# A decoder layer on one core: FFN groups that ran ahead alternate with others, a transposed row of scales through DRAM, B11 kept where T1 will stand, and the last product in single banks

## The chip, the cores and the metric

The kernel runs on one core of one Trainium2 chip. The metric is the device time of one execution in microseconds (us). Engines are named as the profile names them: PE (TensorE, matmuls; PEld its weight loads), DVE (VectorE), ACT (ScalarE), POOL (GpSimd), SP (SyncE, which only issues DMAs here).

## The reference

The layer works on 1024 tokens of width 1024 in float32.

```python
h = rmsnorm(x, pre_mix_g[l])
z = jnp.einsum('btd,dc->btc', h, w_in[l])
q_p, f_p, i_p, g_p, gate_b, gate_c, conv_h = jnp.split(z, split_pts, axis=-1)
mix_a = hgrn2_mixer(q_p, f_p, i_p, g_p, lb_all[l], hgrn_norm_g[l])
mix_b = gate_b * causal_dwconv(gate_c * conv_h, conv_w[l])
mix = jnp.einsum('btc,cd->btd', jnp.concatenate([mix_a, mix_b], axis=-1), w_out[l])
x = x + rmsnorm(mix, post_mix_g[l])
h = rmsnorm(x, pre_ffn_g[l])
u = causal_dwconv(jnp.einsum('btd,df->btf', h, ffn_w_up[l]), ffn_conv_w[l])
gate, val = jnp.split(u, 2, axis=-1)
y = jnp.einsum('btf,fd->btd', jax.nn.silu(gate) * val, ffn_w_down[l])
x = x + rmsnorm(y, post_ffn_g[l])
```

`rmsnorm` multiplies each token by the reciprocal root of its mean square and by a gain. The FFN has 2816 gate and 2816 value columns.

## The kernel before

**Precision.** Every float32 operand of a matmul is split into a high part (a cast, on ACT as a rule, L113) and a low part (a subtraction, on DVE, L114). A product is then three matmuls: high by high, low by high, high by low (`mm3_fm` L167 to L169, `mm3_tm` L172 to L174). Names that begin with h are high parts, those with l low parts.

**Mixing stages, in two halves of 512 tokens.** `gemm_quad` computes four feature tiles of a projection at once in four PSUM banks of pool `ps_mm`: first f0 (forget gate of half 0), then q0, i0, g0, the convolution branch `z_conv` and so on. The scale of each token (`rstd`, a chain of small DVE operations L147 to L155) is not needed before the banks are read out: `evac_f` multiplies each bank of f0 by `rb`, the scales spread over all partitions. For half 0, `stats_by_feature` sums squares with matmuls into `pc`, `rstd` follows, and `by_token` spreads the four columns of scales: four diagonal matrices `dg` on DVE, four matmuls `pb` on PE, one copy `rb` on ACT. These `pb` matmuls stand inside the f0 product. POOL casts the masks `m_diag` and `m_lev` meanwhile. For half 1, `stats` sums squares on ACT and `by_token_through_dram` writes the scales to DRAM and reads them back in transposed order, both on SP.

**FFN up.** It is a Strassen-Winograd scheme over 22 groups of columns, each with seven products. The function `head_1` and `head_2` compute the first two; for the eight groups of `AHEAD` these were computed earlier (`ahead`) and `take_back` loads the result. The other five products are named here by their left operands c2, c1, c7, c4 and c3 (`c2h` the high part). The products c2, c1 and c7 of a group all read one right operand `t` of three parts (`h_t`, `l_t`), which has a single buffer; c4 and c3 read `h_b`, `l_b`. Each product is 12 matmuls. The gate half gathers in PSUM tile `pG`, the value half in `pV`. After c2 and after c7 ACT copies the gate half to `s` (L749), which is added to `pV` on DVE; c4 writes over the place that the second copy reads. The loop at L893 runs one group's `take_back` or `head_1`, then of the group before c4 (`tail_1`), then `head_2`, then c3 (`tail_2`), then c2, c1, c7 of the group (`mid`). `AHEAD = 8` means groups 0 to 7.

**FFN down.** Again seven products, in the order 1, 2, 6, 7, 5, 3, 4, over 22 rows of 128 of which each product sees 11, cut into six granules `GR` of two rows or one. `down_granule` loads the left operand `s` and `right_operand` the right one; blocks B11, B12, B21, B22 of the weight come from `w_dn`, and T1 = B12 - B11, T2 = B22 - T1, T3 = B22 - B12 are made on DVE. The first two granules of product 1 (`EARLY`) were made before. Products alternate between the four banks `bx` and the four banks `by`. Within a granule the row blocks c go (0, 1), then (2, 3). Product 4 is the last; its last three granules are `joined`, so that blocks 0 and 1 end before blocks 2 and 3.

**The end.** `result` squares a block on ACT (`jy`) and multiplies it by the gain on DVE (`my`); `finish_rows` runs `rstd` over the blocks it is given and adds the residual (L1037), then SP stores.

The order of instructions on each engine is fixed when the program is built: a list scheduler places them from the code's order and its own estimates, and `tc.high_priority()` moves a part forward.

Of the kernel before, what the change touches and what calls it, by code (L numbers as in the profile page):

```python
# [17 lines left out]
P = 128  # L18
# [23 lines left out]
def decoder_kernel(ctx: ExitStack, tc: tile.TileContext, x, xT, w_sq, w_cv, w_out, w_up, w_dn,  # L42
# [27 lines left out]
    nc.vector.tensor_scalar(neg[:], vec[:, V_PREF : V_PREF + KH], -1.0, None, ALU.mult)  # L70
# [414 lines left out]
    def z_conv(hf, act, rb, rates, at_end):  # L485
        res = []
        rates = list(rates)
        for j in range(4):
# [23 lines left out]
            if j == 3 and at_end is not None:  # L512
                at_end()
# [99 lines left out]

    first = {}

    def scale_a():
        for _ in hgen:
            pass
        nc.sync.dma_start(ident[:], ident_d)
        with tc.high_priority():  # L620
            first["r"] = stats_by_feature()

    def scale_a_rows():
        with tc.high_priority():
            first["rows"] = by_token(0, first["r"])
# [26 lines left out]
    def ma_tiles(hf):  # L652
# [44 lines left out]
    AHEAD = 8  # L697
# [149 lines left out]
    ahead((AHEAD - 1, 0), {0: box[0]["f"]})  # L847
# [87 lines left out]
    def raw_w(kh, nh, i, n, name):  # L935
        t = ft("wr", (P, 2, TH), name, 5)
# [6 lines left out]
    def t_1(gi, n, b11, b12):  # L943
        t = ts[1, gi] = t_slot(1, gi, n)
        nc.vector.tensor_tensor(t[:], b12[:, :n], b11[:, :n], ALU.subtract)

    def right_operand(op, gi, i, n):

        nm = f"{op}_{gi}"
        if op == 1:  # L950
            b = raw_w(0, 0, i, n, f"b11_{nm}")
            t_1(gi, n, b, raw_w(0, 1, i, n, f"b12_{nm}"))
            return b
        if op == 2:
# [16 lines left out]
        return ts[{5: 1, 6: 2, 7: 3}[op], gi]  # L971
# [163 lines left out]
```

## Time and profile before

| | |
|---|---|
| median of 3 runs | 1138.54 us (1137.28 to 1140.52) |
| the profiled execution | 1138.99 us, of which its span is 1137.2 us |
| mean granted TensorE clock | 0.994 of full |
| PE busy | 1109.6 us, 98% of the span |
| DVE, ACT, POOL busy | 838.4, 512.6 and 9.7 us |
| chain that ended last | PE 86%, DVE 6%, DMA 3%, ACT 3%, issue 2% |

Times in the trace count from the start of the span. Busy time of PE counts a matmul from its start to its modelled end, and these overlap; what PE loses is therefore read from the distance between two starts, and from idle time in front of an instruction together with what ended it.

### The profile page before, as it was taken

What the parts mean: (1) busy time and instruction counts of PE and PEld (TensorE: products, weight loads), DVE (VectorE), ACT (ScalarE), POOL (GpSimd) and SP (SyncE); (2) the same over time, 40 slices, a digit from 0 to 9 for tenths busy, and PEclk for the clock granted to TensorE, in tenths of its full rate; (3) what the DMA queues carried; (4) which work ended last, traced back from release to release, by engine and by line L of the source; (5) the groups of instructions that cost most, each with busy time, mean ns of one, the idle gap of its engine ahead of it and who ended that gap; (6) DMA issues with size and microseconds to landing.
All of it is one profiled execution on the core that took longest, in us unless ns stands there. A gap on an engine that the chain in (4) does not pass through costs nothing.

```text
span 1137.2 us, 13444 instructions
## 1 busy us (share of the span) xinstructions
PE 1109.6 (98%) x5096; PEld 912.8 (80%) x5096; DVE 838.4 (74%) x1181; ACT 512.6 (45%) x750; POOL 9.7 (1%) x16
## 2 busy tenths in 40 slices
PE   8999999999999999999999999999999999999996
PEld 6878888888878888887777888888888877888884
DVE  8578767636687777387998987878887777744786
ACT  6543335425432337366555444444444433544441
POOL 2000000000000000000000000000000000000000
PEclk9999999999999999999999999999999999999998
DMA  8522223335322238174444323222331479735653
GB/s 292 172 78 74 75 93 113 119 95 201 101 66 86 82 111 260 59 256 167 164 168 168 111 94 139 102 75 102 131 110 51 153 282 334 280 102 168 202 165 132
DMA packets 54432, 163.03 MB, mean 143 GB/s; under 512 B 5856, under 2 KB 6112, under 8 KB 51424
## 3 DMA queue, kind: packets, MB, share of 16 engines
q1 hardware_dynamic: 53936, 161.57, 41.5%
q8 instruction: 40, 0.66, 0.2%
q10 hardware_dynamic: 432, 0.61, 0.2%
q14 instruction: 24, 0.20, 0.1%
HBM read 127.82 MB, written 34.34 MB: 143 GB/s over the span
## 4 chain that ended last, share of the span: by engine, by line
PE 86%; DVE 6%; DMA 3%; ACT 3%; issue 2%; DVEq 0%; SPq 0%; ACTq 0%
PE pG L167 8%; PE pG L169 8%; PE pG L168 8%; PE pV L167 4%; PE pV L169 4%; PE pV L168 4%; PE sl L382 2%; PE p_wo L174 2%; PE p_wo L173 2%; PE p_wo L172 2%; DMA b<-w_dn 2%; PE pXv L173 2%; PE pXv L174 1%; PE pXv L172 1%; PE p_ch L169 1%
## 5 line engine op out<-in xcount | busy, mean ns | idle before, releaser
L113 ACT CAST hs<-s 128x1024 fp32r<-128x1024 f32 (+1 forms) x40 | 39.1, 976 | 91.9 <-PE pXg L173 35.9
L114 DVE TENSOR_TENSOR ls<-s,hs 128x1024 fp32r<-128x1024 f32 (+1 forms) x40 | 45.2, 1129 | 44.4 <-ACT hs L113 44.2
L114 DVE TENSOR_TENSOR l_b<-w,h_b 128x1024 fp32r<-128x1024 f32 x22 | 26.9, 1223 | 33.6 <-ACT h_b L113 33.6
L167 PE MATMUL pG<-uhi,h_x 128*128 128x512 f32 x112 | 44.4, 396 | 0.0
L168 PE MATMUL pG<-ulo,h_x 128*128 128x512 f32 x112 | 44.3, 395 | 0.0
L169 PE MATMUL pG<-uhi,l_x 128*128 128x512 f32 x112 | 44.1, 394 | 0.0
L749 ACT COPY s<-pG 128x512 f32<-128x512 f32 x44 | 25.7, 583 | 40.8 <-PE pG L169 40.6
L114 DVE TENSOR_TENSOR l_t<-t,h_t 128x1536 fp32r<-128x1536 f32 x22 | 38.6, 1755 | 5.9 <-ACT h_t L113 5.7
L811 ACT ACTIVATE g<-pG,vec 128x1024 f32<-128x1024 f32 x22 | 24.5, 1116 | 34.2 <-PE pG L169 34.2
L167 PE MATMUL pG<-c4h,h_b 128*128 128x512 f32 x88 | 35.4, 402 | 4.7 <-ACT s L749 4.7
L820 ACT ACTIVATE g<-g 128x1024 f32<-128x1024 f32 x22 | 23.3, 1061 | 36.3 <-DVE g L813 36.1
L113 ACT CAST h_t<-t 128x1536 fp32r<-128x1536 f32 x22 | 32.6, 1484 | 14.4 <-DVE t L783 9.6
L113 ACT CAST h_x<-w 128x1024 fp32r<-128x1024 f32 x14 | 14.7, 1052 | 47.4 <-DMA w<-w_up 47.4
L383 DVE COPY_PREDICATED S<-m_lev,sl 128x512 f32<-128x512 uint8 x28 | 24.9, 890 | 14.7 <-PE sl L382 14.7
L369 ACT COPY lhs<-UW 128x512 f32<-128x512 f32 x28 | 18.6, 663 | 37.2 <-DVE UW L390 37.2
L382 PEld LDWEIGHTS sl<-UW,lhs 128*128 128x128 f32 x224 | 28.8, 190 | 7.3 <-issue 4.1
L169 PE MATMUL pG<-c4h,l_b 128*128 128x512 f32 x88 | 34.6, 393 | 0.0
L167 PE MATMUL pV<-c3h,h_b 128*128 128x512 f32 x88 | 34.5, 392 | 0.0
L167 PE MATMUL pG<-c7h,h_t 128*128 128x512 f32 x88 | 34.4, 391 | 0.1
L169 PE MATMUL pV<-c3h,l_b 128*128 128x512 f32 x88 | 34.4, 391 | 0.0
L169 PE MATMUL pG<-c7h,l_t 128*128 128x512 f32 x88 | 34.3, 390 | 0.0
L168 PE MATMUL pG<-c4l,h_b 128*128 128x512 f32 x88 | 34.3, 390 | 0.0
(351 smaller groups left out, 3524.1 us busy)
## 6 DMA issues: line engine op xcount, KB each, us to landing
w<-w_up SPq DMA_DIRECT2D x22, 1024.0 KB, 4.8
s<-s_d SPq DMA_DIRECT2D x33, 512.0 KB, 3.9
b<-w_dn SPq DMA_DIRECT2D x33, 512.0 KB, 6.0
s_d<-g SPq DMA_DIRECT2D x22, 512.0 KB, 2.9
s_d<-S SPq DMA_DIRECT2D x11, 768.0 KB, 3.4
r_wo<-w_out SPq DMA_DIRECT2D x16, 512.0 KB, 3.5
xT<-xT SPq DMA_DIRECT2D x16, 256.0 KB, 4.0
r_q<-w_sq SPq DMA_DIRECT2D x8, 512.0 KB, 4.3
```

Source lines behind the costliest of these rows:

```text
L113: nc.scalar.copy(hi, src)
L114: nc.vector.tensor_tensor(lo, src, hi.bitcast(F32), ALU.subtract)
L167: nc.tensor.matmul(ps, whi, ahi, start=first, stop=False, skip_group_check=more)
L168: nc.tensor.matmul(ps, whi, alo, start=False, stop=False, skip_group_check=more)
L169: nc.tensor.matmul(ps, wlo, ahi, start=False, stop=last, skip_group_check=more)
L172: nc.tensor.matmul(ps, ahi, whi, start=first, stop=False, skip_group_check=more)
L173: nc.tensor.matmul(ps, ahi, wlo, start=False, stop=False, skip_group_check=more)
L174: nc.tensor.matmul(ps, alo, whi, start=False, stop=last, skip_group_check=more)
L382: nc.tensor.matmul(pv[:, :, i], lhs[:, i, :], rhs, start=True, stop=True)
L383: nc.vector.copy_predicated(view(S, 2 * X, o + h, (X - h, 2), (2 * h, n), (1, h)), m_lev[:, li].rearrange("p x g (b h) -> p x (g b) h", h= ...
L749: nc.scalar.copy(t[:], ps)
L811: nc.scalar.mul(a[:], c, wc[2])
```

## The change

1. **Scales by token.** `by_token` now transposes the four columns of scales on PE in one matmul (`pc<-ident,rs_x`), copies the 4x128 result on ACT, writes it to DRAM on ACT's DMA queue and reads it back to all partitions on POOL's. The product q0 stands in banks of the other pool (`banks=aux`), and `evac_f` is called from inside it. The masks load after the third weight tile of q0. `stats(1)` moves into `z_conv`.
2. **FFN up.** The groups computed ahead are 0, 1, 3, 5, 7, 9, 11, 13; where the next group is one of them, the code writes c3 and then c4 of the group before, without a head between.
3. **FFN down.** Product 1 loads B11 alone, into the slot of T1; product 2 loads B12 and B21 and subtracts in place; T2 is made in product 6 and T3 in product 7, from blocks loaded there again. `wr` has 8 buffers for 5, `sr` 6 for 4. `bx` is all of pool `ps_g`, `by` all of `ps_v`.
4. **The end.** Product 4 adds up in four single banks `pZ`, into which ACT first copies `s3`; its last four granules are joined, and each row block is finished by itself (`last_rows`). `finish_rows(0)` is written ahead of product 4.

```diff
-    def by_token(hf, r):
-
-        pb = aux(f"pb{hf}", (P, NC_H, C))
-        dg = cv(f"dg{hf}", shape=(P, NC_H, C))
-        for c in range(NC_H):
-            nc.vector.tensor_scalar(dg[:, c, :], ident[:], r[:, c : c + 1], None, ALU.mult)
-            nc.tensor.matmul(pb[:, c, :], ones[:], dg[:, c, :], start=True, stop=True)
+    def by_token(hf, r, ps):
+
+        nc.tensor.transpose(ps, r[:], ident[:])
+        t = zt("rt", (NC_H, C), name=f"rt{hf}")
+        nc.scalar.copy(t[:], ps)
+        rd = dp.tile([NC_H, C], F32, name=f"rd{hf}")
+        nc.scalar.dma_start(rd, t[:])
         rb = zt("rb", (P, TH), name=f"rb{hf}")
-        nc.scalar.copy(rb[:], pb.rearrange("p c t -> p (c t)"))
+        nc.gpsimd.dma_start(rb[:], rd.rearrange("c p -> (c p)").partition_broadcast(P))
         return rb
...
-    pss = gemm_quad(w_sq[0], Lazy(), "f0", False, (1, 1, 1, 1, 1, 1, 1, 1), pieces=2, queue=nc.scalar,
-                    hooks={6: scale_a, 7: scale_a_rows})
+    def scale_a_rows():
+        nc.scalar.activation(warm[:], first["r"][:, 0:1], AF.Sigmoid)
+        first["FU"] = evac_f(0, pss, first["rows"])
+
+    pss = gemm_quad(w_sq[0], Lazy(), "f0", False, (1, 1, 1, 1, 1, 1, 1, 1), pieces=2, queue=nc.sync,
+                    hooks={6: scale_a})
     r0 = first["r"]
+    qss = gemm_quad(w_sq[1], act_a, "q0", False, PAIRS, hooks={0: scale_a_rows}, banks=aux)
...
-    AHEAD = 8
+    AHEAD = (0, 1, 3, 5, 7, 9, 11, 13)
...
         if n and not last:
             mid_weights(n)
-        if n:
-            tail_1(n - 1)
-        if n >= AHEAD and not last:
-            head_2(n)
-        if n:
-            tail_2(n - 1)
+        if n and n in AHEAD:
+            product_3(n - 1)
+            product_4(n - 1)
+            gate(n - 1)
+            value(n - 1)
+        elif n:
+            product_4(n - 1)
+            gate(n - 1)
+            if not last:
+                head_2(n)
+            product_3(n - 1)
+            value(n - 1)
...
+        if op <= 2 and (op == 1) == (gi >= EARLY):
+            ts[1, gi] = t_slot(1, gi, n)
+            nc.sync.dma_start(ts[1, gi][:], w_dn[0, 0, :, i : i + n])
         if op == 1:
-            b = raw_w(0, 0, i, n, f"b11_{nm}")
-            t_1(gi, n, b, raw_w(0, 1, i, n, f"b12_{nm}"))
-            return b
+            return ts[1, gi]
         if op == 2:
             b = raw_w(1, 0, i, n, f"b21_{nm}")
             b12 = raw_w(0, 1, i, n, f"b12_{nm}")
-            if gi < EARLY:
-                t_1(gi, n, raw_w(0, 0, i, n, f"b11_{nm}"), b12)
+            nc.vector.tensor_tensor(ts[1, gi][:], b12[:, :n], ts[1, gi][:], ALU.subtract)
+            return b
+        if op == 6:
             b22 = raw_w(1, 1, i, n, f"b22_{nm}")
-            t2 = ts[2, gi] = t_slot(2, gi, n)
-            t3 = ts[3, gi] = t_slot(3, gi, n)
-            nc.vector.tensor_tensor(t2[:], b22[:, :n], ts[1, gi][:], ALU.subtract)
-            nc.vector.tensor_tensor(t3[:], b22[:, :n], b12[:, :n], ALU.subtract)
+            ts[2, gi] = t_slot(2, gi, n)
+            nc.vector.tensor_tensor(ts[2, gi][:], b22[:, :n], ts[1, gi][:], ALU.subtract)
+            return ts[2, gi]
+        if op == 7:
+            b12 = raw_w(0, 1, i, n, f"b12_{nm}")
+            b = raw_w(1, 1, i, n, f"b22_{nm}")
+            nc.vector.tensor_tensor(b[:, :n], b[:, :n], b12[:, :n], ALU.subtract)
             return b
...
-            for cs in ((0, 1), (2, 3)):
+            for cs in ((0,), (1,), (2,), (3,)) if len(gis) > 1 else ((0, 1), (2, 3)):
...
+                if len(gis) > 1 and done:
+                    done(cs[0])
...
-    down_product(4, bx, joined=3)
     finish_rows(0, range(NC_H))
-    for cs in ((0, 1), (2, 3)):
-        for c in cs:
-            result(1, 0, c, bx[c])
-        finish_rows(1, cs)
+
+    def last_rows(c):
+        result(1, 0, c, bz[c])
+        finish_rows(1, [c])
+
+    down_product(4, bz, joined=4, done=last_rows)
```

How this stands in the instruction streams is shown at three places. The first is PE in FFN up, at the end of the c7 product of group 2, with its `pG` (`pG_4533` before, `pG_4537` in the change); `h_t_4670` and `l_t_4671` are the right operand of group 3, `h_b_4630` and `h_b_4656` belong to group 2. Before:

```order
L167 MATMUL pG_4533<-c7h,h_t_4541 128x512
L168 MATMUL pG_4533<-c7l,h_t_4541 128x512
L169 MATMUL pG_4533<-c7h,l_t_4542 128x512
L167 MATMUL pG_4533<-c4h,h_b_4630 128x512
L168 MATMUL pG_4533<-c4l,h_b_4630 128x512
L169 MATMUL pG_4533<-c4h,l_b_4631 128x512
```

In the change:

```order
L167 MATMUL pG_4537<-c7l,h_t_4555 128x512
L168 MATMUL pG_4537<-c7h,l_t_4556 128x512
L166 MATMUL pG_4662<-c2h,h_t_4670 128x512
L167 MATMUL pG_4662<-c2l,h_t_4670 128x512
L166 MATMUL pV_4708<-c1h,h_t_4670 128x512
L166 MATMUL pG_4537<-c4h,h_b_4656 128x512
L167 MATMUL pG_4537<-c4l,h_b_4656 128x512
L168 MATMUL pG_4537<-c4h,l_b_4657 128x512
L166 MATMUL pV_4613<-c3h,h_b_4656 128x512
```

Two c2 matmuls and one c1 matmul of group 3 now stand directly behind the last c7 matmul of group 2, ahead of c4 and c3 of group 2. The same three stand there between groups 4 and 5, 6 and 7, 8 and 9, 10 and 11, and 12 and 13; between 0 and 1 c4 follows c7 as before, and between an odd group and the next even one 12 head matmuls stand ahead of c4.

The second place is ACT at the same point of the program, with the two copies `s` and the cast `h_t` of the next group. Before (groups 2 and 3):

```order
L749 COPY s_2_4600<-pG_4533 128x512
L820 ACTIVATE g_4557<-g_4557 128x1024
L776 COPY pG_4636<-f_4634 128x1024
L749 COPY s_2_4627<-pG_4533 128x512
L113 CAST h_t_4644<-t_4640 128x1536
```

In the change (groups 4 and 5; `h_x` is the operand of the head of group 6):

```order
L112 CAST h_b_4880<-w_4755 128x1024
L741 COPY s_4_4850<-pG_4761 128x512
L112 CAST h_t_4894<-t_4890 128x1536
L741 COPY s_4_4877<-pG_4761 128x512
L112 CAST h_x_4981<-w_4979 128x1024
```

The cast `h_t` of the next group now stands ahead of the second copy instead of behind it.

The third place is DVE towards the end, in product 4: the residual sums of half 0 (`my`, with `xr`) and the low parts of the last two granules (`ls_4`, `lw_4`, `ls_5`, `lw_5`). Before:

```order
L1037 SCALAR_TENSOR_TENSOR my_1_7167<-my_1_7167,rs_y_8499,xr_8523 128x512
L1037 SCALAR_TENSOR_TENSOR my_2_7168<-my_2_7168,rs_y_8499,xr_8527 128x512
L114 TENSOR_TENSOR ls_4_8418<-s_4_8412,hs_4_8417 128x1024
L114 TENSOR_TENSOR lw_4_8422<-b_4_4_8414,hw_4_8421 128x1024
L1037 SCALAR_TENSOR_TENSOR my_2_7168<-my_2_7168,rs_y_8499,xr_8531 128x512
L1037 SCALAR_TENSOR_TENSOR my_3_7169<-my_3_7169,rs_y_8499,xr_8535 128x512
L1037 SCALAR_TENSOR_TENSOR my_3_7169<-my_3_7169,rs_y_8499,xr_8539 128x512
L114 TENSOR_TENSOR ls_5_8431<-s_5_8425,hs_5_8430 128x1024
L114 TENSOR_TENSOR lw_5_8435<-b_4_5_8427,hw_5_8434 128x1024
```

In the change:

```order
L1045 SCALAR_TENSOR_TENSOR my_2_7152<-my_2_7152,rs_y_8305,xr_8337 128x512
L1045 SCALAR_TENSOR_TENSOR my_3_7153<-my_3_7153,rs_y_8305,xr_8341 128x512
L1045 SCALAR_TENSOR_TENSOR my_3_7153<-my_3_7153,rs_y_8305,xr_8345 128x512
L113 TENSOR_TENSOR ls_4_8455<-s_4_8449,hs_4_8454 128x1024
L113 TENSOR_TENSOR lw_4_8459<-b_4_4_8451,hw_4_8458 128x1024
L113 TENSOR_TENSOR ls_5_8468<-s_5_8462,hs_5_8467 128x1024
L113 TENSOR_TENSOR lw_5_8472<-b_4_5_8464,hw_5_8471 128x1024
```

All eight residual sums of half 0 now stand ahead of the low parts of both granules, where five of them stood ahead of the first pair and three ahead of the second.

## Rows read from the trace of the kernel before

**Rows 1.** The page: busy us (share) xinstructions; a DMA group's KB, us to landing.

```profile
PE 1109.6 (98%) x5096; PEld 912.8 (80%) x5096; DVE 838.4 (74%) x1181; ACT 512.6 (45%) x750; POOL 9.7 (1%) x16
...
b<-w_dn SPq DMA_DIRECT2D x33, 512.0 KB, 6.0
```

**Rows 2.** Waits of PE: waiter, waited for, us in total, times, longest.

```profile
PE pG L167 <- ACT s L749: 4.7, 7, 0.7
...
PE pb L278 <- DVE dg L277: 1.9, 1, 1.9
```

**Rows 3.** Windows: length, busy us (instructions) of each engine, PE clock, DMA share, GB/s.

```profile
925.00:980.00 55.00, 51.74 (x214) 40.31 (x213) 41.84 (x39) 23.45 (x28) 0.00 (x0) 0.97 0.94 352
980.00:1126.00 146.00, 146.00 (x646) 120.81 (x644) 91.47 (x119) 62.71 (x88) 0.00 (x0) 1.00 0.50 159
...
955.00:960.00 5.00, 4.58 (x13) 3.63 (x14) 4.43 (x6) 1.24 (x2) 0.00 (x0) 0.66 0.83 267
...
26.00:36.00 10.00, 8.13 (x40) 6.57 (x39) 7.35 (x17) 8.87 (x14) 2.02 (x5) 1.00 0.85 287
```

**Rows 4.** Timeline of PE around `pb`: start us, length us, instruction, [idle before].

```profile
26.16 0.39 PE L168 MATMUL p_f<-lo,h_f 128*128 128x512 f32 x1
...
26.61 0.39 PE L167 MATMUL p_f<-hi,h_f 128*128 128x512 f32 x1
28.87 1.16 PE L278 MATMUL pb<-dg,ones 128*128 128x128 f32 x8 [1.87 <-DVE dg L277]
29.78 0.48 PE L168 MATMUL p_f<-lo,h_f 128*128 128x512 f32 x1
```

**Rows 5.** Timeline of DVE and POOL there: the chain of `rstd` of half 0, mask casts.

```profile
23.75 0.16 DVE L147 TENSOR_SCALAR rt_x<-pc 128x4 f32<-128x4 f32 x1
23.95 0.52 DVE L150 TENSOR_SCALAR rs_x<-rt_x 128x4 int32<-128x4 int32 x1
...
28.53 0.88 DVE L277 TENSOR_SCALAR dg<-ident,rs_x 128x128 f32<-128x128 f32 x4 [0.33 <-DVE rs_x L155]
...
23.84 3.96 POOL L642 CAST m_lev<-mf 128x512 uint8<-128x512 f32 x7
```

**Rows 6.** Timeline of DVE: first and last of the ten operations of `rstd`, half 1.

```profile
42.14 0.16 DVE L147 TENSOR_SCALAR rt_x<-ssx 128x4 f32<-128x4 f32 x1
...
43.92 0.16 DVE L155 SCALAR_TENSOR_TENSOR rs_x<-rt_x,rs_x 128x4 f32<-128x4 f32 x1
```

**Rows 7.** Timeline of PE and ACT between two FFN groups (one of seven alike).

```profile
590.23 0.39 PE L169 MATMUL pG<-c7h,l_t 128*128 128x512 f32 x1
...
590.66 0.58 ACT L749 COPY s<-pG 128x512 f32<-128x512 f32 x1 [2.92 <-PE pG L169]
591.14 1.49 ACT L113 CAST h_t<-t 128x1536 fp32r<-128x1536 f32 x1
...
591.29 0.50 PE L167 MATMUL pG<-c4h,h_b 128*128 128x512 f32 x1 [0.68 <-ACT s L749]
```

**Rows 8.** Timeline of the end: last matmul, ACT, DVE.

```profile
1125.91 0.39 PE L174 MATMUL pXg<-hw,ls 128*128 128x512 f32 x1
...
1127.19 0.68 DVE L1022 TENSOR_TENSOR my<-pXg,pg 128x512 f32<-128x512 f32 x1
...
1129.24 0.16 DVE L147 TENSOR_SCALAR rt_y<-ssy 128x2 f32<-128x2 f32 x1
...
1131.40 2.74 DVE L1037 SCALAR_TENSOR_TENSOR my<-my,rs_y,xr 128x512 f32<-128x512 f32 x4
```

**Rows 9.** Timeline of DVE and ACT in product 4.

```profile
1094.50 1.28 DVE L1024 TENSOR_TENSOR my<-pYv,ds 128x512 f32<-128x512 f32 x2
...
1105.92 3.40 DVE L1037 SCALAR_TENSOR_TENSOR my<-my,rs_y,xr 128x512 f32<-128x512 f32 x5
1109.24 1.22 DVE L114 TENSOR_TENSOR ls<-s,hs 128x1024 fp32r<-128x1024 f32 x1
...
1107.07 1.06 ACT L113 CAST hs<-s 128x1024 fp32r<-128x1024 f32 x1 [4.29 <-PE pXg L173]
```

More of the change, by code (lines that the diff above doesn't have):

```diff
@@ L184, in gemm_quad @@
     def gemm_quad(src, act, name, token_major, groups, order=None, pieces=1, rate=1, hooks=None, queue=None,
-                  gains=None):
+                  gains=None, banks=None):
         order = order or list(range(len(act)))
-        pss = [ps_mm.tile([P, TH], F32, tag="mm", name=f"p_{name}_{j}") for j in range(4)]
+        pss = [banks(f"p_{name}_{j}") if banks else ps_mm.tile([P, TH], F32, tag="mm", name=f"p_{name}_{j}")
+               for j in range(4)]
         ws, i0 = {}, 0
@@ L511, in z_conv @@
             psb = gemm_tile(w_cv[3 * j + 2], act, f"gb{n}")
-            if j == 3 and at_end is not None:
-                at_end()
+            if at_end and j >= 2:
+                at_end[j - 2]()
             tick(rates.pop(0))
@@ L612, in __getitem__ @@
             return act_a[k]
+    lbt = zp.tile([P, 4, H], F32, name="lbt")
+    lbp = vec[:, V_LB : V_LB + H]
+    e_, s_, lb, oml = (lbt[:, i, :] for i in range(4))
+    nc.vector.tensor_tensor(e_, lbp, lbp, ALU.subtract)
+    nc.scalar.activation(e_, e_, AF.Exp)
+    nc.vector.reciprocal(s_, e_)
+    nc.vector.tensor_tensor(s_, s_, e_, ALU.mult)
+    nc.vector.tensor_tensor(lb, s_, s_, ALU.subtract)
+    nc.vector.tensor_scalar(oml, lb, -1.0, 1.0, ALU.mult, ALU.add)
     first = {}
@@ L620, in scale_a @@
         with tc.high_priority():
-            first["r"] = stats_by_feature()
+            pc = aux("pc", (P, NC_H + P))
+            for c in range(NC_H):
+                nc.tensor.matmul(pc[:, c : c + 1], sums[0][:, c * C : (c + 1) * C], ones[:, 0:1], start=True, stop=True)
+            first["r"] = rstd(pc[:, :NC_H], D, "x0")
+            first["rows"] = by_token(0, first["r"], pc[:NC_H, NC_H:])
     def scale_a_rows():
-        with tc.high_priority():
-            first["rows"] = by_token(0, first["r"])
-    pss = gemm_quad(w_sq[0], Lazy(), "f0", False, (1, 1, 1, 1, 1, 1, 1, 1), pieces=2, queue=nc.scalar,
-                    hooks={6: scale_a, 7: scale_a_rows})
+        nc.scalar.activation(warm[:], first["r"][:, 0:1], AF.Sigmoid)
+        first["FU"] = evac_f(0, pss, first["rows"])
+    pss = gemm_quad(w_sq[0], Lazy(), "f0", False, (1, 1, 1, 1, 1, 1, 1, 1), pieces=2, queue=nc.sync,
+                    hooks={6: scale_a})
     r0 = first["r"]
-    rb0 = first["rows"]
+    qss = gemm_quad(w_sq[1], act_a, "q0", False, PAIRS, hooks={0: scale_a_rows}, banks=aux)
+    rb0, (F0, UW0) = first["rows"], first["FU"]
     rq0 = for_values(0, r0)
-    F0, UW0 = evac_f(0, pss, rb0)
-    pss = gemm_quad(w_sq[1], act_a, "q0", False, PAIRS)
-    evac_q(0, pss, rb0, UW0)
+    evac_q(0, qss, rb0, UW0)
     for i in range(2):
@@ L715, in ahead @@
                     nc.sync.dma_start(f_d[n], to[i])
-    for n in range(1, AHEAD - 1, 2):
-        ahead((n, n + 1), {})
+    for i in (1, 3, 5):
+        ahead(AHEAD[i : i + 2], {})
     tick(len(fill))
@@ L846, in decoder_kernel @@
     mid_weights(0)
-    ahead((AHEAD - 1, 0), {0: box[0]["f"]})
+    ahead((AHEAD[-1], 0), {0: box[0]["f"]})
     comb = (P, KH, TH)
@@ L890, in decoder_kernel @@
     ps_v = ctx.enter_context(tc.tile_pool(name="ps_v", bufs=2, space=PSUM, reuse_waits="tile"))
-    ps_g = ctx.enter_context(tc.tile_pool(name="ps_g", bufs=2, space=PSUM, reuse_waits="tile"))
+    scope_g = ExitStack()
+    ps_g = scope_g.enter_context(tc.tile_pool(name="ps_g", bufs=2, space=PSUM, reuse_waits="tile"))
     for n in range(NF + 1):
         last = n == NF
-        if n >= AHEAD and not last:
+        if n not in AHEAD and not last:
             head_weights(n)
             head_1(n)
-        elif n < AHEAD:
+        elif not last:
             take_back(n)
@@ L1057, in decoder_kernel @@
     s3 = keep(bx, "ds3_")
+    scope_g.close()
+    ps_d = ctx.enter_context(tc.tile_pool(name="ps_d", bufs=4, space=PSUM, reuse_waits="tile"))
+    bz = [ps_d.tile([P, TH], F32, tag="mm", name=f"pZ{c}")[:] for c in range(NC_H)]
+    for c in range(NC_H):
+        nc.scalar.copy(bz[c], s3[c][:])
     down_product(5, by, True)
```

68 lines of the change are left out of this document (24 added, 44 removed).

## The prediction

> **What bounds the kernel now.** I read the page first: PE is busy for 1109.6 of 1137.2 us [rows 1], so nothing counts that doesn't shorten PE's work, a gap in it, or the stretch behind its last matmul. The number of matmuls hardly changes, so I looked for gaps. The windows give the rate: from 980 to 1126 us PE never idles and starts 646 matmuls in 146.00 us, 0.226 us each [rows 3]. In the view of PE's waits three things lie where the change works: seven waits for the copy `s` in FFN up, one for `dg` near the start [rows 2], and the stretch from 925 to 980, where 214 matmuls need 48.4 us of 55 at that rate [rows 3]. Then comes the end: the last matmul starts at 1125.91 [rows 8], 11.3 us before the span ends. Profiled time and span differ by 1.8 us, and the profiled 1138.99 lies 0.45 above the median of 1138.54; I sum against the profiled time and quote against the median.
>
> **Start.** Between the starts of the matmul ahead of `pb` and of the one behind it lie 3.17 us (26.61 to 29.78 [rows 4]); without `pb` it would be 0.23, so this spot costs 2.94. PE waits because the chain of ten small operations runs from 23.75 to 28.20 (28.53 less 0.33 [rows 5]): 0.52 us for an operation while the mask casts run on POOL, where half 1's chain, alone, took 0.16 for each and 1.94 us in all (42.14 to 43.92 plus 0.16 [rows 6]). In the change the masks land later, and POOL's own order has only `m_diag` and one `m_lev` ahead of an operation that needs the scales, so the other six casts fall behind. The chain then ends at 23.75 + 1.94 = 25.7, and with 0.33 to the next engine the transpose could start at 26.0. It stands two matmuls earlier than `pb`, behind the one of 26.16, so at 26.4: no wait. The transpose isn't in this trace; eight small `pb` instructions took 1.16 [rows 4], so it costs 0.15 at least and 0.5 at most. If `m_diag` and one `m_lev` still fall into the chain, it loses up to 1.8 us (five operations by 0.36). Gain 0.6 to 2.8; I take 2.4.
>
> The row `rb` now comes through two DMAs. Their cover is q0, whose banks are its own: 96 matmuls, 21.7 us. On DVE the readout of f0 waits for `rb`, and behind it stand the low parts of q0's fourth weight tile, needed 72 matmuls (16.3 us) into q0. q0 starts 22 matmuls behind the transpose, about 31.7; the tile is due at 48, and with some 6 us of readout and split before it, `rb` may land at 42, 15 us after the transpose. A copy and two DMAs at the slowest median landing of the page, 6.0 [rows 1], fit. I take zero.
>
> The Trainium skill ("SBUF — State Buffer", section "SBUF: two separate sides") says that VectorE and GpSimd share one pair of ports under an exclusive lock, which agrees with 0.52 against 0.16 above. It also says there that a DMA from GpSimd's queue can't have its descriptors written while VectorE holds the lock, which speaks against reading `rb` on that queue; no run here shows it. By it the gain would still stand, since ahead of the readout DVE has only two splits left, and then waits for `rb` itself.
>
> **FFN up.** Seven times PE goes from c7 straight to c4 and waits for the second copy `s`: the last c7 starts at 590.23, c4 at 591.29 [rows 7], 1.06 for 0.23, so 0.83 lost each time and 5.8 in all. With a head of 12 matmuls (2.7 us) between, the wait is covered. The change puts a head between c7 and c4 wherever an odd group meets an even one; the meeting of 0 and 1 keeps its 0.83.
>
> Where an even group meets an odd one (six times) the order of PE in the change shows something else: c2, c2 and c1 of the next group directly behind c7. They need the next `h_t`. That tile has one buffer, and c7 reads it, so the cast can't start before the last matmul that reads it, `c7l,h_t`, the one before the last. That the reader alone releases is seen in the down product: the cast `hs` at 1107.07 was ended by L173, low by high, not by L174 behind it [rows 9]. The cast takes 1.49 [rows 7]. In the times of rows 7: copy `s` started 0.43 after the start of the matmul it waited for, so the cast starts at 590.00 + 0.43, ends at 591.92, and PE resumes 0.05 later at 591.97 instead of 590.46. That is 1.51 lost. On ACT the second copy stands behind this cast and ends at 592.4, when PE is still at the three early matmuls (to 592.65): c4 doesn't wait again. c3 needs the sum of the copy on DVE, 0.7 later: just in time. So FFN up loses 0.83 + 6 x 1.51 = 9.9 for 5.8: **+4.1**. Bounds: -5.0 if no cast is in the way, +6.2 if the cast `h_x`, ahead of `h_t` on ACT at two of the six meetings, adds 1.05 to each.
>
> **FFN down.** From 925 to 980 PE loses 55 - 48.4 = 6.6 us at most; the clock was at 0.66 in 955 to 960 [rows 3], 1.7 us of it. DMA moved 352 GB/s at a share of 0.94 there. Over products 1 and 2 the diff cuts loads: of the weight, product 1 reads 1.75 MB for 3.5, product 2 6.5 for 9.25. With `s` product 2 had 12 MB in 11 x 12 matmuls (29.9 us), 400 GB/s, more than was moved; now it has 9.25 MB, 310 GB/s. Products 6 and 7 get 2.75 and 5.5 MB more: 180 and 280 GB/s with `s`, under 352 too. The subtractions are as many as before. So the late loads should go, and the low clock, which stands behind those waits, with them. I take 5.0 of the 6.6 gained; bounds 0 (the loads stay late) and 6.6.
>
> **The end.** Before, the last matmul is followed by two blocks of `result` (`my` at 1127.19, the second 1.4 later, `rstd` from 1129.24), the chain, and four residual sums from 1131.40, 2.74 long [rows 8]. With one block the chain starts 0.6 behind the first `my` (two of them took 1.28 [rows 9]), at 1127.8, one of its operations done ahead: 1.97; then two sums, 1.37: done at 1131.1 for 1134.1. Gain 3.0. The block before is through by then: blocks now end 21 matmuls (4.75 us) apart, and DVE's work for one is about 4.
>
> But the joined stretch needs granules 4 and 5 sooner. It begins when granule 1 ends, near 1107.1 (cast `hs` of 1107.07 [rows 9]), and each block takes nine matmuls to reach granule 4: 1109.1. DVE's order in the change has the results of product 3 (from 1094.5 [rows 9], eight operations and two small splits, 0.6 apart: 6.1), the chain (2.4), all eight residual sums (0.67 apart, as five took 3.40: 5.3) and only then `ls_4`, `lw_4`, `ls_5`, `lw_5` (1.14 apart, 1.22 long). `lw_4` is done at 1110.6 for 1109.4, `lw_5` at 1112.9 for 1112.0 then. PE loses 1.3 and 0.9; product 3's results may start 0.3 earlier, since a subtraction that waited for a load is gone ahead of them. I take **2.0 lost**, bounds 0 and 3. Net 1.0 gained.
>
> **Other edits.** `stats(1)` in `z_conv`, the scales of half 1 over other queues, the moved `neg` and table loads, the four copies into `pZ`: zero, beside PE's stream with many us until they are needed.
>
> **Sum.** -2.4 + 4.1 - 5.0 - 1.0 = -4.3: 1134.7 against the profiled time, **1134.2** against the median.
>
> **The rivals.**
> - *The alternation works*: `h_t` is ready at once, FFN up gains 5.0. Time 1134.2 - 9.1 = 1125.1. For: with a head between, nothing waits in the later groups. Against: one buffer, and PE's order. Chance 0.13.
> - *Slower, the clock*: after each of the six waits PE's clock falls to its half level, as in 955 to 960 at 0.66 [rows 3], 1.4 to 1.7 us each. 6 x 1.5 = 9.0: 1143.2, slower. Against: a single wait of 1.87 near the start [rows 4] left the clock at 1.00 from 26 to 36 [rows 3], and a meeting comes once in 33 us. From the third fall on it eats up the 4.3; with all six it can be told from no change. Chance 0.08.
> - *Down loads stay late*, since their slots come free no sooner: -5.0 is missing, 1139.2. For: the first loads can't start before FFN up frees memory. Chance 0.13.
> - *`rb` late*, past 42 us: 1 us for each us, say 1138. Chance 0.06.
>
> **How the numbers follow.** The forecast has the other 0.60. Its own range, from 1.8 either way at the start, 2.1 more in FFN up, 2 in the joined stretch and 1.6 in the down stage, is 1130.5 to 1138. The range of 8 in 10 reaches towards the alternation and late loads: 1128.0 to 1140.0. It leaves out the alternation and the clock. A measurement here tells 0.3% (3.4 us) from no change: faster means below 1135.1. The forecast is below in 0.36 of its 0.60, the alternation wholly, late loads and `rb` in 0.04: faster 0.53. Slower is above 1142: the clock's 0.08. The rest, 0.39, is the same.
>
> **What would show it.** Right: PE waiting on ACT `h_t` six times for about 1.3 us idle between 530 and 740, and once on `s`; no wait for `dg`, chain operations of 0.16; no wait for `hw` or `lw` from 925 to 980; waits for `lw` in product 4 about 18 and 16 us before the end of matmuls; some 8 us between last matmul and end. Wrong: a clock below 1.00 behind the `h_t` waits, `tf` starting past 42, loads of `T` landing after 928.

## The result, and the profile after

The changed kernel takes 1129.4 us (median of 4 executions, 1128.56 to 1130.54), against 1139.53 for the kernel before (median of 4, 1137.28 to 1143.21). The ratio is 0.9909, with a 95% interval from 0.988 to 0.9938: faster by some 10 us, where the forecast was 4.3. Of the kernel with 12 warm matmuls below, one execution of 1774.78 us at a mean granted clock of 0.584 is left out. The profiled execution of the changed kernel took 1128.56 us, with a span of 1126.7. The row of its page that answers to the first of [rows 1]:

```profile
PE 1103.9 (98%) x5090; PEld 910.6 (81%) x5090; DVE 839.1 (74%) x1199; ACT 511.2 (45%) x755; POOL 10.0 (1%) x18
```

The waits of PE in it (waiter, waited for, us in total, times, longest). Line numbers in this file differ from those of before by a few (L166 to L168 and L171 to L173 are now the three matmuls, L112 and L113 cast and subtraction):

```profile
PE pG L166 <- ACT h_t L112: 6.7, 5, 1.3
...
PE pG L166 <- DVE S L835: 1.3, 1, 1.3
...
PE pG L166 <- ACT s L741: 0.7, 1, 0.7
...
PE pZ L172 <- DVE lw L113: 0.2, 1, 0.2
```

Against [rows 2], the wait for `dg` is gone, and so are all waits for `hw` and `lw` in products 1 and 2. The seven waits for `s` have become one, and six new ones of 1.3 us idle stand there instead: five are put down to `h_t`, and the sixth, at the same place of its group, to an operation on DVE that happened to end late.

Four marks in both traces split the gain. Until the first matmul of `q0` the changed kernel is ahead by 4.65 us (29.80 for 34.45). From there to the first matmul of product 2 it takes 908.88 us for 906.40, 2.48 more: FFN up loses 4.0 more, and gaps of 1.5 in product 1 are gone. From there to the last matmul it takes 179.84 for 185.06, 5.22 less, and from the start of the last matmul to the end 8.21 for 11.29, 3.08 less. The four make -10.47.

**Start.** DVE's chain of scales and what POOL, PE and DVE do about it, in the changed kernel (start, length, instruction, [idle before]):

```profile
21.98 0.16 DVE L146 TENSOR_SCALAR rt_x<-pc 128x4 f32<-128x4 f32 x1 [0.16 <-PE pc L610]
...
23.31 0.61 POOL L632 CAST m_lev<-mf 128x512 uint8<-128x512 f32 x1
23.42 0.52 DVE L152 TENSOR_TENSOR rt_x<-rt_x 128x4 f32<-128x4 f32 x1
...
24.17 0.16 DVE L154 SCALAR_TENSOR_TENSOR rs_x<-rt_x,rs_x 128x4 f32<-128x4 f32 x1
24.43 0.39 PE L167 MATMUL p_f<-lo,h_f 128*128 128x512 f32 x1
24.66 0.27 PE L257 MATMUL pc<-ident,rs_x 128*4 128x128 f32 x1
24.68 0.48 PE L168 MATMUL p_f<-hi,l_f 128*128 128x512 f32 x1
25.00 0.40 PE L166 MATMUL p_f<-hi,h_f 128*128 128x512 f32 x1
...
28.11 0.73 POOL L263 DMA_DIRECT2D rb<-rd  x1 [3.47 <-DMA rd<-rt]
...
35.75 2.48 DVE L279 TENSOR_TENSOR tf<-p_f,rb 128x512 f32<-128x512 f32 x4 [2.99 <-DMA rb<-rd]
```

Only one operation of the chain took 0.52 for 0.16, under the mask cast of 23.31, where in [rows 5] most of the chain did. It runs from 21.98 to 24.33: 2.35 us for 4.45. PE doesn't wait for the transpose, which puts two matmuls 0.57 apart (24.43 to 25.00) that would stand 0.46 apart without it: 0.11. `rb` lands at 35.7, six us ahead of the 42 that the prediction allowed.

**FFN up**, between groups 2 and 3, on PE and ACT:

```profile
560.84 0.39 PE L167 MATMUL pG<-c7l,h_t 128*128 128x512 f32 x1
...
561.07 0.39 PE L168 MATMUL pG<-c7h,l_t 128*128 128x512 f32 x1
561.27 1.47 ACT L112 CAST h_t<-t 128x1536 fp32r<-128x1536 f32 x1 [4.20 <-PE pG L167]
...
562.65 0.58 ACT L741 COPY s<-pG 128x512 f32<-128x512 f32 x1
...
562.79 0.50 PE L166 MATMUL pG<-c2h,h_t 128*128 128x512 f32 x1 [1.34 <-ACT h_t L112]
...
563.13 0.39 PE L167 MATMUL pG<-c2l,h_t 128*128 128x512 f32 x1
...
563.36 0.40 PE L166 MATMUL pV<-c1h,h_t 128*128 128x512 f32 x1
```

From 561.07 to 562.79 are 1.72 us for 0.226: 1.50 lost. The cast was released by L167, the last reader of the old `h_t`, 0.43 behind its start (561.27 - 560.84), and not by L168. The same loss of 1.50 stands at 595.59, 630.10, 664.62, 699.13 and 733.64, and the one wait for `s`, at 527.00, loses 0.84.

**Down.** Two windows of the changed kernel (length, busy us of PE, PEld, DVE, ACT and POOL, PE clock, DMA share, GB/s); the second answers to the first of [rows 3]:

```profile
8.00:12.00 4.00, 4.00 (x19) 3.29 (x19) 4.00 (x8) 4.00 (x8) 0.00 (x0) 1.00 1.00 358
925.00:980.00 55.00, 55.00 (x245) 45.53 (x244) 39.92 (x40) 24.85 (x31) 0.00 (x0) 1.00 1.02 400
```

245 matmuls for 214, at a clock of 1.00 for 0.97. Nothing is lost in these 55 us. The first window comes up below.

**The end.** DVE and PE in the joined stretch of product 4, which begins at 1099.15, and at the end:

```profile
1094.78 5.39 DVE L1045 SCALAR_TENSOR_TENSOR my<-my,rs_y,xr 128x512 f32<-128x512 f32 x8
...
1100.09 1.22 DVE L113 TENSOR_TENSOR ls<-s,hs 128x1024 fp32r<-128x1024 f32 x1
...
1101.23 1.22 DVE L113 TENSOR_TENSOR lw<-b,hw 128x1024 fp32r<-128x1024 f32 x1
...
1101.88 0.39 PE L173 MATMUL pZ<-hw,ls 128*128 128x512 f32 x1
...
1102.50 0.50 PE L172 MATMUL pZ<-lw,hs 128*128 128x512 f32 x1 [0.24 <-DVE lw L113]
...
1118.52 0.39 PE L173 MATMUL pZ<-hw,ls 128*128 128x512 f32 x1
...
1119.72 0.69 DVE L1030 TENSOR_TENSOR my<-pZ,pg 128x512 f32<-128x512 f32 x1 [0.81 <-ACT jy L1029]
1120.33 0.15 DVE L148 SCALAR_TENSOR_TENSOR rt_y<-ssy,rt_y 128x1 f32<-128x1 f32 x1
...
1122.26 1.41 DVE L1045 SCALAR_TENSOR_TENSOR my<-my,rs_y,xr 128x512 f32<-128x512 f32 x2
```

The tail is that of the forecast, with two residual sums for four [rows 8]. In the joined stretch DVE came as forecast (all eight sums, then the low parts), but PE lost 0.40 at 1101.88 (0.62 for 0.226), 0.11 on the matmul behind it, and nothing else.

### The profile page after: what moved, and what is told of

The parts are those of the page before. It is cut to its first block, busy times and chain, and to the rows that moved or that the text cites. A ratio compares the mean times of both kernels' runs of the same rounds, so it can differ in the third digit from the quotient of the medians.

```text
span 1126.7 us, 13472 instructions
## 1 busy us (share of the span) xinstructions
PE 1103.9 (98%) x5090; PEld 910.6 (81%) x5090; DVE 839.1 (74%) x1199; ACT 511.2 (45%) x755; POOL 10.0 (1%) x18
## 4 chain that ended last, share of the span: by engine, by line
PE 88%; DVE 5%; ACT 4%; DMA 2%; issue 1%; DVEq 0%; SPq 0%; ACTq 0%
PE pG L166 7%; PE pG L167 7%; PE pG L168 7%; PE pV L166 3%; PE pV L168 3%; PE pV L167 3%; PE pX L171 3%; PE pX L173 3%; PE pX L172 3%; PE pY L171 2%; PE pY L172 2%; PE pY L173 2%; PE sl L358 2%; PE p_wo L173 2%; PE p_wo L171 2%; PE p_wo L172 2%
## 5 line engine op out<-in xcount | busy, mean ns | idle before, releaser
L113 DVE TENSOR_TENSOR ls<-s,hs 128x1024 fp32r<-128x1024 f32 (+1 forms) x40 | 45.2, 1129 | 44.9 <-ACT hs L112 44.9
L112 ACT CAST hs<-s 128x1024 fp32r<-128x1024 f32 (+1 forms) x40 | 39.1, 977 | 73.4 <-PE pY L172 31.2
L172 PE MATMUL pY<-lw,hs 128*128 128x512 f32 x132 | 51.3, 389 | 0.0
L173 PE MATMUL pY<-hw,ls 128*128 128x512 f32 x132 | 51.3, 389 | 0.0
L171 PE MATMUL pY<-hw,hs 128*128 128x512 f32 x132 | 51.2, 389 | 0.0
L112 ACT CAST h_t<-t 128x1536 fp32r<-128x1536 f32 x22 | 32.6, 1481 | 38.5 <-PE pG L167 35.8
L113 DVE TENSOR_TENSOR l_t<-t,h_t 128x1536 fp32r<-128x1536 f32 x22 | 38.6, 1756 | 9.6 <-ACT h_t L112 9.6
L171 PE MATMUL pX<-hw,hs 128*128 128x512 f32 x116 | 45.1, 389 | 0.0
L172 PE MATMUL pX<-lw,hs 128*128 128x512 f32 x116 | 45.1, 389 | 0.0
L173 PE MATMUL pX<-hw,ls 128*128 128x512 f32 x116 | 45.1, 389 | 0.0
L166 PE MATMUL pG<-uhi,h_x 128*128 128x512 f32 x112 | 44.4, 396 | 0.0
L167 PE MATMUL pG<-ulo,h_x 128*128 128x512 f32 x112 | 44.3, 395 | 0.0
L168 PE MATMUL pG<-uhi,l_x 128*128 128x512 f32 x112 | 44.1, 394 | 0.0
L166 PE MATMUL pG<-c2h,h_t 128*128 128x512 f32 x88 | 34.9, 396 | 8.0 <-ACT h_t L112 6.7
L804 DVE SCALAR_TENSOR_TENSOR v<-pV,vec,v 128x1023 f32<-128x1023 f32 x22 | 28.2, 1280 | 18.0 <-ACT v L803 17.9
L113 DVE TENSOR_TENSOR l_b<-w,h_b 128x1024 fp32r<-128x1024 f32 x22 | 26.8, 1220 | 17.3 <-ACT h_b L112 17.3
L803 ACT ACTIVATE v<-pV,vec 128x1024 f32<-128x1024 f32 x22 | 24.5, 1112 | 26.6 <-PE pV L168 26.5
L166 PE MATMUL pG<-c4h,h_b 128*128 128x512 f32 x88 | 34.8, 395 | 0.7 <-ACT s L741 0.7
```

Of the source, the lines that this page charges most:

```text
L112: nc.scalar.copy(hi, src)
L113: nc.vector.tensor_tensor(lo, src, hi.bitcast(F32), ALU.subtract)
L166: nc.tensor.matmul(ps, whi, ahi, start=first, stop=False, skip_group_check=more)
L167: nc.tensor.matmul(ps, whi, alo, start=False, stop=False, skip_group_check=more)
L168: nc.tensor.matmul(ps, wlo, ahi, start=False, stop=last, skip_group_check=more)
L171: nc.tensor.matmul(ps, ahi, whi, start=first, stop=False, skip_group_check=more)
```

## The experiments

The theory after this result: each part of the change works by the mechanism that the prediction names, the alternation against the others; the down loads were sized too small and the joined stretch too large. The rivals: the alternation pays somewhere else; the larger gain at the start belongs to the change; the late low parts cost their 2 us after all. Kernels that carry one part alone are the kernel before with that part of the change.

**The alternation undone**, in the changed kernel:

```diff
-    AHEAD = (0, 1, 3, 5, 7, 9, 11, 13)
+    AHEAD = 8
...
-        if n and n in AHEAD:
-            product_3(n - 1)
-            product_4(n - 1)
...
+        if n:
+            tail_1(n - 1)
+        if n >= AHEAD and not last:
+            head_2(n)
+        if n:
+            tail_2(n - 1)
```

> The changed kernel with AHEAD and the loop of before (groups 0 to 7 run ahead, c4 then c3), all else as changed. Theory (the cast h_t of the next group costs 1.50 us at each of six meetings, the copy s 0.84 at one, against seven times 0.84 before): the waits fall from 9.8 to 5.9 us, so 4.0 faster than the changed kernel, about 1125.4 us, span 1122.7; seven waits of c4 for s, none for h_t. Rival (the alternation gains elsewhere, by a DVE that is less full, and the waits only stand for that): slower than the changed kernel, 1130 to 1134.

1125.95 us (1124.78 to 1127.96), ratio 0.9872 [0.9853, 0.989] to the kernel before; span 1123.0, 3.7 below that of the whole change. Its waits of PE:

```profile
PE pG L166 <- ACT s L741: 4.7, 7, 0.7
```

The seven waits of [rows 2] are back, no wait for `h_t` is left, and the kernel is faster. The alternation costs, and by the forecast amount.

**The alternation alone**, on the kernel before (the same lines, the other way round):

> The kernel before with the second part alone (groups 0, 1, 3, 5 to 13 run ahead, and the loop of the change). Theory: six waits of c2 for h_t of 1.50 us and one of c4 for s of 0.84 in place of seven of 0.84: 4.0 slower than before. Rival (the six waits stand only where the start or the later stages of the change put them): the same or faster than before.

1144.31 us (1143.11 to 1146.98) for 1140.73 of before, ratio 1.0034 [1.0021, 1.0046]: slower by 3.6. Its waits:

```profile
PE pG L167 <- ACT h_t L113: 6.7, 5, 1.3
...
PE pG L167 <- DVE S L843: 1.3, 1, 1.3
```

**The right operand `t` in two tiles**, so that c2 has one of its own, in the changed kernel:

```diff
-        b["t"] = parts(t[:], ("th", "tl"), (P, 3, KH, P), f"_t{n}")
+        b["t0"] = parts(t[:, 0:1], ("th0", "tl0"), (P, 1, KH, P), f"_t0{n}")
+        b["t"] = parts(t[:, 1:3], ("th", "tl"), (P, 2, KH, P), f"_t{n}")
...
-        product(a, b["t"], 0, 6)
+        product(a, b["t0"], 0, 6)
```

> The changed kernel, with the operand t split into two tiles, one for c2 alone and one for c1 and c7, each cast and subtracted by itself. The first can be cast while c7 of the group before still reads the second. Theory (one buffer, read by c7, is what holds c2 up): the six waits of 1.50 us go, and the seven c2 matmuls ahead of c4 (1.6 us) cover the cast of the second tile (1.05) and the copy s behind it (0.58); only the 0.84 between groups 0 and 1 stays. 9.0 faster than the changed kernel: about 1120.4, span 1117.7. Rival (ACT is late by itself, by the order of its queue, whatever the buffers): waits of over 1 us stay in front of c2 or c4, 1127 to 1130.

1121.74 us (1121.69 to 1121.95), ratio 0.9833 [0.9817, 0.9849]. PE and ACT between groups 2 and 3:

```profile
563.26 0.39 PE L168 MATMUL pG<-c7h,l_t 128*128 128x512 f32 x1
...
563.46 1.06 ACT L112 CAST h_t<-t 128x1024 fp32r<-128x1024 f32 x1 [3.93 <-PE pG L167]
563.49 0.39 PE L166 MATMUL pG<-c2h,h_t 128*128 128x512 f32 x1
...
564.42 0.57 ACT L741 COPY s<-pG 128x512 f32<-128x512 f32 x1
...
565.08 0.47 PE L166 MATMUL pG<-c4h,h_b 128*128 128x512 f32 x1
```

c2 follows c7 after 0.23 us, since its operand was cast when the c2 matmuls before had read it; the cast of the other two, 1.06 for 1.47 long, lies beside PE; and c4 waits for nothing. So it was the one buffer of `h_t`, read to the end of c7, that made the six waits. With that mended the alternation is worth 4.2 us (1125.95 - 1121.74), near the 5.0 of the rival in which it works. The span is 1119.7 for the 1117.7 expected; its start held a stretch at half rate (below), and `q0` began at 31.40 and not 29.80.

**Part 1 alone**, the scales through DRAM and `q0` in other banks, on the kernel before:

```diff
-        pb = aux(f"pb{hf}", (P, NC_H, C))
...
+        nc.tensor.transpose(ps, r[:], ident[:])
...
+        nc.scalar.dma_start(rd, t[:])
...
+        nc.gpsimd.dma_start(rb[:], rd.rearrange("c p -> (c p)").partition_broadcast(P))
```

> The kernel before with the first part of the change alone (all that stands ahead of FFN up: queue of the first weights, scales by token, q0 in its own banks, stats of half 1 in the convolution branch). Theory A (the half clock from 7.8 to 11.2 us is gone because of these edits): q0 starts 4.65 earlier than before, time about 1134.9. Theory B (the clock there is a matter of the run): the wait for dg and pb are gone, 3.0, and the clock at 8 to 12 us is 0.63 in this profile, or 1.00 and then also in kernels whose start is that of before; time about 1136.5.

1136.65 us (1134.86 to 1137.59) for 1140.52, ratio 0.9964 [0.9951, 0.9976]. From the first `pc` matmul to `q0` it takes 8.80 us, as the whole change does, for 11.78 before: the mechanism is worth 2.98. The other 1.67 of the 4.65 belong to the window from 8 to 12. First the kernel before, then part 1 alone:

```profile
8.00:12.00 4.00, 4.00 (x13) 3.14 (x12) 2.39 (x6) 4.00 (x8) 0.00 (x0) 0.63 0.81 287
```

```profile
8.00:12.00 4.00, 4.00 (x12) 3.07 (x11) 4.00 (x7) 4.00 (x8) 0.00 (x0) 0.62 1.02 363
```

12 or 13 matmuls for 19, 0.43 us apart and not 0.23, at a granted clock of some 0.6, so mostly at 1.2 GHz of 2.4. Part 1 doesn't remove this; it comes with the run.

**Part 3 alone**, the down loads, on the kernel before:

```diff
-        t = ft("wr", (P, 2, TH), name, 5)
+        t = ft("wr", (P, 2, TH), name, 8)
...
+        if op <= 2 and (op == 1) == (gi >= EARLY):
+            ts[1, gi] = t_slot(1, gi, n)
+            nc.sync.dma_start(ts[1, gi][:], w_dn[0, 0, :, i : i + n])
...
-        s = ft("sr", (P, 2, TH), f"s{op}_{gi}", 4)
+        s = ft("sr", (P, 2, TH), f"s{op}_{gi}", 6)
```

> The kernel before with the loads of the down product alone changed (right_operand with B11 in the slot of T1, wr of 8 buffers, sr of 6); banks, end, FFN up and start as before. Theory (the late loads of products 1 and 2 cost all of the gaps from 925 to 980, clock included): 6.0 faster than before, about 1133.5; no wait of PE for hw or lw there, clock 1.00. Rival (a part of the 6 comes from the banks bx and by being whole pools, or the loads stay late for want of memory): gaps of 2 us or more stay, 1135.5 to 1139.

1133.44 us (1132.2 to 1135.72), ratio 0.9938 [0.9922, 0.9954]: 7.1 gained. The window that answers to [rows 3]:

```profile
925.00:980.00 55.00, 55.00 (x244) 45.53 (x244) 38.05 (x37) 23.91 (x29) 0.00 (x0) 1.00 1.01 395
```

The whole loss of the stretch goes with this part: from 895 us to the last matmul no two matmuls in a row start more than 0.28 us apart, where the kernel before lost 7.0 us. It holds fewer loads in products 1 and 2 and also more buffers; which of the two does it wasn't tried.

**Part 4 alone**, the end, on the kernel before:

```diff
-    down_product(4, bx, joined=3)
...
+    def last_rows(c):
+        result(1, 0, c, bz[c])
+        finish_rows(1, [c])
+
+    down_product(4, bz, joined=4, done=last_rows)
```

> The kernel before with the last part of the change alone (product 4 in single banks pZ, four granules joined, each row block finished by itself, rows of half 0 finished ahead of product 4; the banks bx and by as in the change). Theory: the stretch from the last matmul to the end falls from 11.3 to 8.2 us, and one wait of PE for lw of some 0.4 us appears in product 4: 2.7 faster than before. Rival (the joined stretch costs as much as was forecast, 2 us, and only other parts of the change hid that): 1.1 faster. The late loads of products 1 and 2 and the seven waits for s stay.

1138.25 us (1136.49 to 1142.15) for 1140.73, ratio 0.9981 [0.9969, 0.9993]: 2.5 gained. From the start of the last matmul to the end it takes 8.16 us, as in the whole change, but PE waits for low parts for nearly 2 us:

```profile
1108.05 1.22 DVE L114 TENSOR_TENSOR lw<-b,hw 128x1024 fp32r<-128x1024 f32 x1
...
1110.36 5.39 DVE L1041 SCALAR_TENSOR_TENSOR my<-my,rs_y,xr 128x512 f32<-128x512 f32 x8
...
1115.88 0.39 PE L172 MATMUL pZ<-hw,hs 128*128 128x512 f32 x1
...
1116.80 1.22 DVE L114 TENSOR_TENSOR lw<-b,hw 128x1024 fp32r<-128x1024 f32 x1
1118.08 0.50 PE L173 MATMUL pZ<-lw,hs 128*128 128x512 f32 x1 [1.81 <-DVE lw L114]
```

1.97 lost (2.20 for 0.226), and some of the matmuls behind it ran 0.43 apart, another 1.6. It isn't the wait of the whole change. Here the low parts of granule 4 stand inside DVE's chain, ahead of the sums (the first line), and PE didn't wait for them; behind all eight sums stand those of granule 5. In both kernels the first pair behind the sums is done 7.66 us after they start. Here they start 5.75 us ahead of the matmul that needs this pair (1116.11, by PE's rate), in the whole change 7.33 ahead (1094.78 for 1102.11); the 1.58 between is the difference of the two waits.

As to the wait the rival is right, and the time, 2.5 with an interval from 0.8 to 3.5, decides between 2.7 and 1.1 for neither. The profile doesn't show where 2.5 come from: from the first matmul of product 4 to the end it takes 41.61 us, for 40.97 before. It is of an execution of 1142.05, the second longest of twelve; whether the shorter ones wait less is open.

**A longer run of `pw`**, the matmuls on `ones` ahead of the first weights, in the kernel of two tiles:

```diff
-WARM = 9
+WARM = 12
```

> The kernel with two tiles for t, with 12 warm matmuls in place of 9 ahead of the first weights (24 instructions for 18), so that PE is busy until about 6.2 us instead of 5.0. Theory (the half clock from 8 to 12 us follows the idle time ahead of the first weight matmul at 6.8, 1.6 to 2.2 us long, and comes in some runs): the idle time is below 1 us, the clock from 8 to 12 is 1.00, and q0 starts at 29.8 and not at 31.4: up to 1.6 faster than with 9, 1120 to 1121.7. Rival (the clock there has nothing to do with that idle time): 0.6 at 8 to 12 us again in the profile.

1120.9 us (median of four, 1120.36 to 1121.42), ratio 0.9827 [0.9811, 0.9843]. The window from 8 to 12 and the first matmuls:

```profile
1.05 5.49 PE L76 MATMUL pw<-ones 128*128 128x128 f32 x24 [1.05 <-DVE pr L475]
6.86 0.47 PE L166 MATMUL p_f<-hi,h_f 128*128 128x512 f32 x1 [0.32 <-DVE h_f L132]
...
8.00:12.00 4.00, 4.00 (x19) 3.32 (x19) 4.00 (x7) 4.00 (x8) 0.00 (x0) 1.00 1.00 362
```

In the profile the stretch at half rate is gone; as it is missing from three of eight profiles with 9 too, one profile doesn't show that the longer run removes it. The time can't be told from that of the two tiles alone.

**With it, the results of half 0 finished inside the end** (the call moved into `last_rows`):

```diff
-    finish_rows(0, range(NC_H))
...
     def last_rows(c):
+        if c == 0:
+            finish_rows(0, range(NC_H))
```

> The same with the rows of half 0 finished inside the joined stretch, so that on DVE one residual sum and not eight stand ahead of ls and lw of granule 4, and six ahead of those of granule 5. Theory (these sums make lw late): the wait of PE for lw in product 4 (0.4 us) goes, 0.4 faster than with 12 warm matmuls, which the profile can show and the time can't. Rival: the wait moves to granule 5, or the finish of block 0 comes late and with it the end.

1120.93 us (1120.42 to 1121.27), ratio 0.9827 [0.9811, 0.9843]. DVE and PE in the joined stretch:

```profile
1086.63 0.75 DVE L1046 SCALAR_TENSOR_TENSOR my<-my,rs_y,xr 128x512 f32<-128x512 f32 x1
...
1088.43 1.22 DVE L113 TENSOR_TENSOR lw<-b,hw 128x1024 fp32r<-128x1024 f32 x1
1089.57 3.40 DVE L1046 SCALAR_TENSOR_TENSOR my<-my,rs_y,xr 128x512 f32<-128x512 f32 x5
...
1093.24 0.39 PE L172 MATMUL pZ<-lw,hs 128*128 128x512 f32 x1
...
1094.02 1.22 DVE L113 TENSOR_TENSOR lw<-b,hw 128x1024 fp32r<-128x1024 f32 x1
...
1095.29 0.50 PE L172 MATMUL pZ<-lw,hs 128*128 128x512 f32 x1 [0.30 <-DVE lw L113]
```

The sums are what made `lw` of granule 4 late: with one sum ahead of it and not eight it ends at 1089.65, and the matmul that needs it starts at 1093.24 without a wait. But as the rival has it, the wait moves to granule 5, whose low parts stand behind six sums and end at 1095.24: PE lost 0.46 there (from 1094.60 to 1095.29, for 0.226), where the kernel with 12 warm matmuls lost 0.42 at granule 4. So the edit gains nothing. The last three kernels can't be told from one another; each beats both the kernel before, by 19 to 20 us, and the changed one, by some 8 (0.9833 and twice 0.9827 for 0.9909).

## Why the prediction was right or wrong

The direction was right: 10.1 us gained for 4.3. The time, 1129.4, is inside the wide range but below the forecast's own 1130.5 to 1138, in the part kept for an alternation that works. It doesn't work, so it is partly luck that the time lies there: two terms were mis-sized the same way. By the traces the terms are -3.0 + 4.0 - 7.0 + 0.5 - 3.1 = -8.6 (start, FFN up, down, joined stretch, tail); the 1.5 left of the 10.1 are open, and about as large as a difference at the start that no edit made (below). The medians of the parts alone sum to -3.9 + 3.6 - 7.1 - 2.5 = -9.9, near the whole, so the parts hardly act on one another; most of what they have over the -8.6 is the start, where part 1 alone gained 3.9 by its median and 3.0 by its mechanism.

- **FFN up, +4.1: right.** Six losses of 1.50 and one of 0.84, for seven of 0.83, make 4.0; undone it gave 3.7 of span, alone it cost 3.6. The mechanism (one buffer, the last reader, PE's order) is shown by the two tiles. That c4 would not wait again is right too.
- **Down, -5.0: mis-sized.** The step "I take 5.0 of the 6.6 gained" kept a rest back for which no row spoke. The loads alone gave 7.1. By the distances between starts the kernel before loses 6.8 us from 925 to 980, slightly more than the 6.6 worked out from a count of matmuls, since a window counts those that reach over its edges too; 0.2 more lie ahead of it, at 920.5 to 921.2. All of it went. The reason given, that 400 GB/s are "more than was moved", doesn't hold as a limit: the changed kernel moved 400 in the same window. Whether fewer bytes or more buffers did it is open.
- **The joined stretch, +2.0: mis-sized, by an oversight.** DVE was timed well: `lw_4` was forecast 3.5 us behind the start of the stretch (1110.6 - 1107.1), and came 3.3 behind it (1102.45 - 1099.15). The step that failed is "each block takes nine matmuls to reach granule 4". In PE's order matmuls of block 1 stand between those of block 0: three ahead of the first that needs `lw_4` (0.68 us), seven by `lw_5` (1.6). The first wait so shrank to 0.4 and the second went. The prediction read the order of DVE there and not that of PE. That sums ahead of the low parts cost PE a wait is right: in part 4 alone it lost 1.97, at granule 5, though the matmul that needs `lw_5` stands thirteen places later there than block by block.
- **The tail, -3.0: right**, 3.08.
- **Start, -2.4: the mechanism right, the size off.** 2.98 in two kernels. The transpose cost 0.11, under the 0.15 to 0.5 allowed, and nothing waited. The two profiles differ by 1.67 more, which is no part of the change: the clock from 8 to 12 was low in one and full in the other. How much of this is in the medians is open; part 1 alone gained 3.9 with the half-rate stretch in its profile, 0.9 more than its mechanism.
- **The rivals.** That the alternation works is refuted. So is the clock, for these waits: behind them the matmuls run at 0.23 (563.13 to 563.36), the granted clock is 1.00 throughout FFN up, and the six waits of the alternation alone are the same. The reason given against it was weak, though. The wait for `dg` near the start, 1.87 in the kernel before, left the clock at 1.00 there; in part 4 alone the same wait, 1.9, is followed by matmuls 0.43 apart at a granted clock of 0.50 from 30 to 33 us, and in the loads alone so is the wait of 2.4 for `mx`, from 449 to 452. Late down loads are refuted by the window, a late `rb` by `tf` at 35.75.

The Trainium skill ("SBUF — State Buffer", section "SBUF: two separate sides") says that VectorE and GpSimd share a pair of ports under a lock. The trace agrees as far as it goes: the operation of the chain that ran beside the cast `m_lev` took 0.52 for 0.16. Its warning that descriptors of a DMA on GpSimd's queue may be held up can't be judged: `rb` arrived 7.6 us behind its issue at 28.11, and no run puts it on another queue.

## What to carry to other kernels

When products are put in another order, look for the operand that the next one needs and count its buffers: an operand with one buffer is free only when its last reader is done, and a cast of 1.5 us then stands bare. Splitting it by reader cost nothing here and turned a loss of 4 us into a gain of 4. A wait that is forecast from one engine's order has to be held against the other's too, instruction by instruction, since a scheduler may have put work of another block between. And a wait that goes at one place may come back at the next: look which granule waits, not only whether one does.

## What the runs showed of the hardware

Matmuls 0.43 us apart somewhere from 7 to 11 us stand in five of the eight profiles of kernels with `WARM = 9`, and in neither of the two with 12. With 9, PE idles 1.4 to 2.3 us between `pw` and the first weights, and the length of that idle doesn't sort the five from the three. Nor does the kernel: of the four with the start of before, loads alone has no such stretch, and of the four with the changed start, the alternation undone and the whole change have none. In two of the five (the alternation alone and part 4 alone) the view gives a clock of 1.00 over matmuls that stand 0.43 apart. There the records of the clock begin at 10.4 and 9.5 us, behind that stretch, and the view puts 1.00 where it has none; the distance of the matmuls is the safer sign. The Trainium skill ("TensorE: Matmul & The Clock Gate", Part 1) says that the number of slow matmuls at a start differs between runs of one kernel. The profiles agree as far as they go: within each of the two starts some have none and others 5 to 8, one profile to a kernel.

The wait of `mt` for `mx` near 440 us lost from 0.4 to 2.5 us in the ten profiles, without any edit near it; its cause is open, and it is as large as several terms of the sum.

Work beside POOL's casts was lengthened on DVE for a large operation too: the low part `l_q` at 30.86 took 1.90 us beside `m_lev`, and 1.22 at 39.85 without it.
